# One table of expert slots in DRAM, results scattered by token and choice

## Chip, core, metric

The kernel runs on one core of a Trainium2 chip. The metric is the device time of one execution in microseconds (us). The core has TensorE (PE; matmuls and transposes into PSUM), VectorE (DVE), ScalarE (ACT), GpSimd (POOL) and SyncE (SP). DMAs are issued from SP, ACT and POOL; those whose rows are chosen by an index (gathers and scatters) are issued from POOL.

## What is computed

A decoder layer for 512 tokens of width 1024. After a mixer (recurrent branch and dilated attention) and a layer norm, a mixture of 32 experts is applied, of which each token uses four; then a layer norm, a gated embedding and a last layer norm. The part that matters here:

```python
def _moe(x, w_router, b_router, w_gate, b_gate, w_up, b_up, w_down, b_down):
    logits = (xt @ w_router).astype(jnp.float32) + b_router.astype(jnp.float32)
    top_v, top_e = lax.top_k(logits, TOP_K)
    gates = jax.nn.softmax(top_v, axis=-1)
    ...
        g = xe @ w_gate[e] + b_gate[e]
        up = xe @ w_up[e] + b_up[e]
        g = jnp.minimum(g, SWIGLU_LIMIT)
        up = jnp.clip(up, -SWIGLU_LIMIT, SWIGLU_LIMIT)
        hdn = (up + 1.0) * (g * jax.nn.sigmoid(SWIGLU_ALPHA * g))
        return hdn @ w_down[e] + b_down[e]
    ...
    y = jnp.zeros((T, D), jnp.float32).at[buf_tok].add(yb.astype(jnp.float32) * buf_w[:, None])
```

## The kernel before

Up to about 650 us stand the mixer, the first layer norm and the router. The normed rows are written to a table `tab` in DRAM. `cum` (32 experts x 512 tokens) holds the running count of each expert's tokens, so that the token in slot i of an expert is the number of tokens whose count is at most i.

The experts are taken in pairs, ranked by their number of tokens: an even place holds up to 128 tokens, an odd ("small") place up to 64, packed so that the high and low halves of the operands share one pass. Every expert has three stages, gate, up and down, of four quarters each (`times`, L1035). A quarter needs a megabyte of weights that ACT and DVE have split into a high and a low part (`split_ahead`, L1001, `hi_lo`, L69); up to four split pairs lie ahead of PE, and each split frees a slot for which SP issues the next load (`load_next`, L635). The stages run in the order up e, gate e+1, down e. Small tasks are hung into the quarters by hand: `plan` (L1294) names a quarter and a task, and the lists `pre` and `post` say whether it is traced ahead of the quarter's split or behind its matmuls. From L1282 on, the instructions of DVE, ACT and PE keep the order in which they are traced; those of POOL and SP are ordered by the scheduler.

Which tokens an expert gets is found expert by expert. `index_mm(e)` (L786) broadcasts the expert's row of `cum` to 128 partitions with one matmul into a PSUM bank; `index(e)` (L790) compares it with the partition's number on DVE and sums, which gives the token of each slot, then casts it to an integer. `gather(e)` (L808) fetches those rows of `tab` with an indirect DMA, two experts ahead of their use (`x_turn`, `x_homes`).

`result(e)` (L1135) copies an expert's output from PSUM to `yh` and writes it to a contiguous block of `yall` in DRAM. The last two experts never go there; their outputs are placed by matmuls with a one-hot matrix (`finish`, `place`). `token_rows` (L1192) computes once, for each token and choice, the row of `yall` that holds its result. At the end `bring` (L1180) gathers, by that row, the results of 128 tokens for one choice at a time (16 indirect DMAs, two to a buffer of 1 MB), and `add` (L1186) adds them into `acc` with their weights: four adds in the last gate stage, four in the last up stage, four in each of the two last down stages (`in_down`, L1417, `in_last`, L1439).

Of the kernel before, what the change touches and what calls it, by code (L numbers as in the profile page):

```python
# [19 lines left out]
S = 512  # L20
# [42 lines left out]
def build(tc, a, out):  # L63
# [29 lines left out]
    dram = top.enter_context(tc.tile_pool(name="dram", bufs=1, space=bass.MemoryType.DRAM))  # L93
    tab = dram.tile([S, D], F32, name="tab")
    gtab = dram.tile([S, E], F32, name="gtab")
    yall = dram.tile([(E // 2 - 1) * (128 + SM), D], F32, name="yall")
    pled = dram.tile([S, D], F32, name="pled")

    phase1 = stack()
# [457 lines left out]
    for p in (0, 64):  # L557
# [10 lines left out]
    V.scalar_tensor_tensor(bdn[96:98], lor[96:98].bitcast(F32), ident[96:98, 97:98], bdn[96:98].bitcast(F32),  # L568
                           op0=OP.mult, op1=OP.add)

    def branch(w, u, src, g, after):
        kt = len(src[1])
        for m in range(2):
            c = slice(m * 128, m * 128 + 128)
            ps = ps_p.tile([128, S], F32, name="pp")
            for k in range(kt):
                mm3(ps, (w[0][:, k, c], w[1][:, k, c]), (src[0][:, k], src[1][k]), k == 0, k == kt - 1)
            V.tensor_tensor(g[2 * u + m], g[2 * u + m], ps, op=OP.mult)
            after(2 * u + m)
# [77 lines left out]
    def bcast(ap, shape):  # L657
        return ap.to_broadcast(shape)
# [119 lines left out]
    def small(e):  # L778
        return e % 2 == 1
# [1 line left out]
    def on_chip(e):  # L781
        return e >= E - 2

    sel, cbs = {}, {}

    def index_mm(e):  # L786
        cbs[e] = ps_y.tile([128, S], F32, name="py")
        T.matmul(cbs[e], bcast(pick[:, e:e + 1], [128, 128]), cum, start=True, stop=True)

    def index(e, cb=None, junk=None):  # L790

        if cb is None:
            cb = junk = cbs.pop(e)
        else:
            T.matmul(cb, bcast(pick[:, e:e + 1] if e else first, [128, 128]), cum, start=True, stop=True)
        pos = mp.tile([128, 1], F32, name="pos", bufs=5)
        V.tensor_scalar(junk, cb, ip2 if small(e) else ip, None, op0=OP.is_le, op1=OP.add, accum_out=pos)
        idx = mp.tile([128, 1], I32, name="idx", bufs=3)
        V.tensor_copy(idx, pos)
        sel[e] = [pos, idx]  # L800

    def fetch(into, src, idx, n=128):

        G.indirect_dma_start(out=into[:n], out_offset=None, in_=src,
                             in_offset=bass.IndirectOffsetOnAxis(ap=idx[:n], axis=0),
                             bounds_check=src.shape[0] - 1, oob_is_err=False)

    def gather(e):  # L808
        idx = sel[e][1]
        if small(e):  # L810
            fetch(xgs, tab, idx, SM)
        else:
            fetch(xg, tab, idx)
        if on_chip(e):
            wtg = mp.tile([128, E], F32, name="wtg", bufs=2)
            G.memset(wtg, 0.0)
            fetch(wtg, gtab, idx)
            sel[e].append(wtg)


    wo = []
# [42 lines left out]
    index(0, ps_r.tile([128, S], F32, name="pg"), rt.tile([128, S], F32, name="xt1", bufs=1))  # L864
    gather(0)


# [205 lines left out]
    def x_homes(e, j):  # L1073

        if j == 0 and on_chip(e):
            wt = mw.tile([128, 1], F32, name="wt")
            junk = mw.tile([128, E], F32, name="oh", bufs=1)
            V.scalar_tensor_tensor(junk, rows[:, 0], float(e), sel[e][2], op0=OP.is_equal, op1=OP.mult, accum_out=wt)
            sel[e][1] = wt
# [52 lines left out]
    def h_small(e):  # L1132
        hT[e] = halves("hh", sg.pop(e), mw)

    def result(e):  # L1135

        ps = psd.pop((e, "d"))
        if small(e):
            y, low = [mw.tile([SM, D], F32, name=name, bufs=1) for name in ("yh", "gs")]
            for h in HS:  # L1140
                A.activation(low[:, h], ps[:, h][SM:], AF.Copy)
            for h in HS:
                V.tensor_tensor(y[:, h], ps[:, h][:SM], low[:, h], op=OP.add)
            G.dma_start(yall[e // 2 * (128 + SM) + 128:e // 2 * (128 + SM) + 128 + SM], y)
        else:
            y = mw.tile([128, D], F32, name="yh", bufs=1)
            for h in HS:
                A.activation(y[:, h], ps[:, h], AF.Copy)
            G.dma_start(yall[e // 2 * (128 + SM):e // 2 * (128 + SM) + 128], y)

    def finish(ps, pos, wt, iS, names=("yh", "gs", "xh")):

# [7 lines left out]
    def down_whole(e, between):  # L1160
        if e == E - 1:
            ps = ps_g.tile([128, D], F32, name="pg")
            names = ("yh", "gs", "xh")
        else:
            ps = TwoBanks([ps_y.tile([128, 512], F32, name="py") for _ in range(2)])
            names = ("hh", "hl", "sg")
        times_whole(ps, hT.pop(e), (e, "d"), between)
        ys[e] = finish(ps, *sel.pop(e)[:2], iS, names)

    def place(ps, e, r, h, first, last):  # L1170

# [8 lines left out]
    def bring(r, k):  # L1180
        n = r * TOP + k
        if n % 2 == 0:
            got[n // 2] = slot(("ringb", "ring")[n // 2 % 2], [128, 2, D])
        fetch(got[n // 2][:, n % 2], yall, yidx[:, n:n + 1])

    def add(r, k):  # L1186
        n = r * TOP + k
        V.scalar_tensor_tensor(acc[:, r], got[n // 2][:, n % 2], evs[:, r, k:k + 1], acc[:, r], op0=OP.mult, op1=OP.add)

    yidx = mp.tile([128, R * TOP], I32, name="yidx")  # L1190

    def token_rows():  # L1192

        cT, far, where = [mw.tile([128, R, E], F32, name=name, bufs=1) for name in ("xh", "hl", "hh")]
        yrow = mw.tile([128, R * TOP], F32, name="gpos", bufs=1)
        tq = ps_y.tile([128, R, E], F32, name="py")
        for r in range(R):  # L1200
            T.transpose(tq[:, r], cum.bitcast(F32)[0:E, r * 128:r * 128 + 128], ident[:E, :E])
        sh = [128, R, E]
        V.tensor_tensor(far, tq, bcast(rows[:, 2:3], sh), op=OP.is_gt)
        V.scalar_tensor_tensor(cT, far, 8192.0, tq, op0=OP.mult, op1=OP.add)
        V.tensor_tensor(cT, cT, bcast(rows[:, 1:2], sh), op=OP.add)
# [4 lines left out]
        V.scalar_tensor_tensor(ev, yrow, yall.shape[0] - 0.5, ev, op0=OP.is_lt, op1=OP.mult)  # L1210
        V.tensor_copy(yidx, yrow)

    def turned_gates():

# [71 lines left out]
        x_homes(0, j)  # L1286
    for _ in range(2):
        split_ahead()
    index_mm(1)
    index(1)  # L1290
    gather(1)
    split_ahead()

    def plan(*tasks):  # L1294

# [24 lines left out]

    gate_mm(0, {}, plan((0, index_mm, 2), (1, index, 2), (1, gather, 2), (2, token_rows), (3, turned_gates)))
    gate_out(0)
    for e in range(E - 1):
        f, last = e + 1, e == E - 2
        pre, post = [], [(1, x_turn, f), (2, gather, e + 2), (2, index_mm, e + 3)]
        if e == 0:
            post = post[:1] + post[2:]
        if e:  # L1330
            pre.append((0, result, e - 1))
        pre.append((2, x_homes, f, 0))
        if not small(f):
            pre.append((3, x_homes, f, 1))
        post = [t for t in post if t[2] < E]
        if last:
            post += [(q, bring, n // TOP, n % TOP) for q in range(4) for n in (2 * q, 2 * q + 1)]
            pre.append((0, first_rows))
        up_mm(e, plan(*pre), plan(*post))

        pre, post = [], []
        if e + 3 < E:
            pre.append((1 if small(e) else 2, index, e + 3))
        if small(e):
            pre += [(0, up_in, e), (2, up_small, e), (3, h_small, e)]
            post += [(0, up_fold, e)]
# [2 lines left out]
            post += [(2, h_turn, e)]  # L1349
        if e == 0:  # L1350
            pre += [(q, scale, q) for q in range(4)]
        if last:
            pre += [(q, add, 0, q) for q in range(4)]
            post += [(q, bring, 2, q) for q in range(4)]
        gate_mm(f, plan(*pre), plan(*post))

        pre, post = [], []
# [6 lines left out]
        if not last:  # L1364
            down_mm(e, plan(*pre), plan(*post))
        else:
            pre += [(q, add, 1, q) for q in range(4)]
            post += [(q, bring, 3, q) for q in range(4)]
            up_mm(f, plan(*pre), plan(*post))

    iS = numbers(xgs[:, 0:S])
# [28 lines left out]

    lns = [ln_rows(("ln2_g", "ln2_b"), "ring2")]
    wg_lo = slot("ring2", WG, F32R)
    plev = rows_of(pled, "ring")
    lns.append(ln_rows(("ln3_g", "ln3_b"), "ring"))
    scratch = slot("ring", [128, 2, D])

    def wg_split(u):
        if u < 2:
            pair = [wp.tile(WG, F32R, name=name) for name in ("whi", "wlo")]
# [7 lines left out]
    def in_down(q):  # L1417
        if q == 0:
            wg_split(0)
        if q == 1:  # L1420
            up_in(E - 1)
            up_fold(E - 1)
            up_small(E - 1)
            hT[E - 1] = halves("xh", sg.pop(E - 1), mr)
        if q == 2:
            wg_split(1)
        add(2, q)

    down_whole(E - 2, in_down)

# [8 lines left out]
    def in_last(q):  # L1439
        if q < 2:  # L1440
            for h in HS:
                bias_rows(sums[q][:, h], q, h)
            wg_split(q + 2)
        elif q == 2:

            A.activation(tiny, epst, AF.Sqrt)
        add(3, q)

    down_whole(E - 1, in_last)


    part = mp.tile([128, 2, R, 2], F32, name="part")
# [132 lines left out]
```

## Time and profile before

| | us |
|---|---|
| median of 3 runs (1870.08 to 1872.62) | 1872.47 |
| the profiled execution | 1869.88 |
| its span, first to last instruction | 1867.7 |
| busy: PE, DVE, ACT, POOL | 1771.9, 1407.6, 1163.3, 151.8 |

Times in the rows count from the span's start. A busy PE is not PE at its peak, since matmuls are pipelined. The chain of waits is followed back from the last instruction, at each step to what released it. Idle time stands in brackets behind an instruction, with what ended it. All calls of DVE, ACT and PE go through one helper and so have line 47; tiles tell them apart. Tiles of the pools `ring` and `ring2` are both shown as ring.

### The profile page before, as it was taken

How to read it: one execution, taken by the hardware profiler on the slowest of the kernel's cores; microseconds unless marked ns; L12 is line 12 of the kernel's file. 1: busy time of each engine (PE TensorE's matmuls, PEld its weight loads, DVE VectorE, ACT ScalarE, POOL GpSimd, SP SyncE). 2: the span in 40 equal slices, each digit the busy share in tenths (PEclk: the TensorE clock that was granted, in tenths of full speed). 3: DMA queues.
4: the chain of work that ended last, by engine and by line, in shares of the span. 5: the costliest groups of instructions: out<-in, count | busy, mean ns of one | idle time of the engine just before them, and what ended most of it. 6: DMA issues, size and time to landing. Idle time of an engine off the chain costs nothing.

```text
span 1867.7 us, 23225 instructions
## 1 busy us (share of the span) xinstructions
PE 1771.9 (95%) x8610; PEld 1458.6 (78%) x8610; DVE 1407.6 (75%) x1473; ACT 1163.3 (62%) x1165; POOL 151.8 (8%) x119
## 2 busy tenths in 40 slices
PE   8999999999999789999999999999999999998898
PEld 7989888888879667777778778778778778777567
DVE  4233333466667598999999999999999999998765
ACT  3233345465533377778778778778778778777334
POOL 1010100000000011001010010000100100112400
PEclk9999999999999899999999999999999999999899
DMA  6322221132346479999999999999999999999931
GB/s 180 91 69 68 69 68 57 49 111 80 99 138 237 167 289 360 378 400 386 382 395 385 395 387 385 390 384 390 395 382 390 386 381 395 378 390 362 356 122 46
DMA packets 138352, 503.03 MB, mean 269 GB/s; under 512 B 11347, under 2 KB 77861, under 8 KB 89076
## 3 DMA queue, kind: packets, MB, share of 16 engines
q1 hardware_dynamic: 127076, 470.62, 66.9%
q0 software_dynamic: 9856, 28.39, 4.1%
q10 hardware_dynamic: 1296, 2.43, 0.3%
q8 instruction: 70, 1.15, 0.3%
q14 instruction: 54, 0.44, 0.1%
HBM read 487.73 MB, written 18.22 MB: 271 GB/s over the span
## 4 chain that ended last, share of the span: by engine, by line
PE 52%; DVE 25%; issue 14%; ACT 5%; DMA 3%; another core or an unknown queue 0%; POOL 0%; DVEq 0%; SPq 0%; ACTq 0%; POOLq 0%
PE pp L47 22%; DVE wlo L47 13%; PE py L47 10%; PE pu L47 8%; PE pg L47 5%; DVE ringb L47 4%; PE pt L47 4%; ACT ringb L47 3%; PE s L47 2%; PE o L47 1%; DVE py L47 1%; DVE pu L47 1%; DVE yh L47 1%; DMA wraw<-in_w_ple_gate_dram 1%; DVE xh L47 1%
## 5 line engine op out<-in xcount | busy, mean ns | idle before, releaser
L47 DVE TENSOR_TENSOR wlo<-ring,whi 128x2048 fp32r<-128x2048 f32 x237 | 537.7, 2285 | 29.0 <-ACT whi L47 28.7
L47 ACT ACTIVATE whi<-ring 128x2048 fp32r<-128x2048 f32 x237 | 449.3, 1915 | 79.6 <-PE pg L47 37.7
L47 DVE TENSOR_TENSOR wlo<-wraw,whi 128x1024 fp32r<-128x1024 f32 (+2 forms) x139 | 225.2, 1626 | 164.1 <-ACT whi L47 164.0
L47 ACT ACTIVATE whi<-wraw 128x1024 fp32r<-128x1024 f32 (+2 forms) x139 | 190.2, 1381 | 129.1 <-PE pp L47 104.4
L47 PE MATMUL pp<-xth,whi 128*128 128x512 f32 x448 | 180.8, 404 | 0.0
L47 PE MATMUL pp<-xtl,whi 128*128 128x512 f32 x448 | 175.4, 391 | 0.0
L47 PE MATMUL pp<-xth,wlo 128*128 128x512 f32 x448 | 174.9, 391 | 0.2 <-DVE wlo L47 0.2
L47 PE MATMUL pu<-whi,xh 128*128 128x512 f32 (+1 forms) x440 | 140.3, 391 | 0.4 <-ACT xh L47 0.4
L47 PE MATMUL pg<-whi,xh 128*128 128x512 f32 (+1 forms) x420 | 134.6, 396 | 4.0 <-ACT whi L47 4.0
L47 PE MATMUL pg<-wlo,xh 128*128 128x512 f32 (+1 forms) x412 | 131.0, 395 | 5.0 <-DVE wlo L47 5.0
L47 PE MATMUL pu<-wlo,xh 128*128 128x512 f32 (+1 forms) x424 | 132.6, 388 | 3.0 <-DVE wlo L47 3.0
L47 DVE TENSOR_TENSOR ringb<-ring,ringb 128x2048 fp32r<-128x2048 f32 x45 | 103.1, 2290 | 30.3 <-ACT ringb L47 30.3
L47 PE MATMUL py<-whi,hh 128*128 128x512 f32 x364 | 118.2, 406 | 2.2 <-DVE hh L47 0.3
L47 PE MATMUL py<-wlo,hh 128*128 128x512 f32 x364 | 115.4, 398 | 1.2 <-DVE wlo L47 1.1
L47 DVE TENSOR_TENSOR ringb<-wraw,ringb 128x2048 fp32r<-128x2048 f32 x46 | 105.2, 2286 | 12.7 <-ACT ringb L47 12.7
L47 PEld LDWEIGHTS pp<-xtl,whi 128*128 128x128 f32 x448 | 84.7, 189 | 19.8 <-issue 2.9
L47 PEld LDWEIGHTS pp<-xth,whi 128*128 128x128 f32 x448 | 84.6, 189 | 18.5
L47 PEld LDWEIGHTS pp<-xth,wlo 128*128 128x128 f32 x448 | 84.3, 188 | 18.6 <-DVE wlo L47 0.7
L47 PEld LDWEIGHTS pg<-wlo,xh 128*128 128x128 f32 x412 | 78.6, 191 | 23.8 <-DVE wlo L47 6.2
L47 PEld LDWEIGHTS pu<-wlo,xh 128*128 128x128 f32 x424 | 79.5, 188 | 22.0 <-DVE wlo L47 4.3
L47 PEld LDWEIGHTS pg<-whi,xh 128*128 128x128 f32 x420 | 78.8, 191 | 21.2 <-ACT whi L47 4.6
L47 PEld LDWEIGHTS pu<-whi,xh 128*128 128x128 f32 x440 | 80.3, 188 | 16.2 <-ACT xh L47 0.6
(422 smaller groups left out, 3419.8 us busy)
## 6 DMA issues: line engine op xcount, KB each, us to landing
ring<-in_w_gate_dram SPq DMA_DIRECT2D x98, 1024.0 KB, 7.3
ring<-in_w_down_dram SPq DMA_DIRECT2D x96, 1024.0 KB, 7.5
ring<-in_w_up_dram SPq DMA_DIRECT2D x94, 1024.0 KB, 7.8
wraw<-in_w_up_dram SPq DMA_DIRECT2D x34, 1024.0 KB, 7.1
wraw<-in_w_down_dram SPq DMA_DIRECT2D x32, 1024.0 KB, 8.7
wraw<-in_w_gate_dram SPq DMA_DIRECT2D x30, 1024.0 KB, 7.5
wraw<-in_w_in_dram SPq DMA_DIRECT2D x18, 1024.0 KB, 5.1
wraw<-in_w_in_dram SPq DMA_DIRECT2D x32, 512.0 KB, 4.2
```

What stands on the lines that cost most here:

```text
L47: ins = method(*args, **kw)
```

## The change

A DRAM table `stab` with one entry for each slot of each expert (16 pairs x 192 slots) is filled with the number 2048, which is no row, and 16 indirect DMAs (`fill`, one for each block of 128 tokens and choice) scatter into it, by the slot's number, the row `token * 4 + choice`. `slot_rows` reads the table back into `slotn`, 128 slots x 32 experts, with three DMAs of four-byte pieces, and one DVE shift makes the tokens, `toks`. `gather` takes its indices from `toks` for experts 4 and up; for 0 to 3 the search stays (`direct`). `token_rows` moves from quarter 2 to quarter 0 of the first gate stage, the fills stand behind quarter 1, `slot_rows` behind quarter 2 of the first up stage.

The results go to `ytok`, one row for each token and choice, which is filled with zeros ahead of the mixer's last products. `store` scatters an expert's output to those rows with an indirect DMA. `bring` becomes a plain DMA of two choices of 128 tokens, 1 MB. The adds move: four in the last up stage, four in the down stage of expert 30, eight in that of expert 31; the loads for the end (`plev`, the last norm's rows) and the scratch buffer come behind that.

```diff
-    yall = dram.tile([(E // 2 - 1) * (128 + SM), D], F32, name="yall")
+    ytok = dram.tile([S * TOP, D], F32, name="ytok")
+    stab = dram.tile([E // 2 * (128 + SM), 1], I32, name="stab")
...
+    zero = bt.tile([128, D], F32, name="zero")
+    G.memset(zero, 0.0)
+    for n in range(S * TOP // 128):
+        G.dma_start(ytok[n * 128:n * 128 + 128], zero)
+    none = bt.tile([128, stab.shape[0] // 128], I32, name="none")
+    G.memset(none, S * TOP)
+    G.dma_start(stab.rearrange("(p n) o -> p (n o)", p=128), none)
...
-    def index_mm(e):
-        cbs[e] = ps_y.tile([128, S], F32, name="py")
-        T.matmul(cbs[e], bcast(pick[:, e:e + 1], [128, 128]), cum, start=True, stop=True)
...
     def gather(e):
-        idx = sel[e][1]
+        idx = sel[e] if e in sel else toks[:, e:e + 1]
...
+    def store(e, y, n):
+        G.indirect_dma_start(out=ytok, out_offset=bass.IndirectOffsetOnAxis(ap=slotn[:n, e:e + 1], axis=0),
+                             in_=y, in_offset=None, bounds_check=S * TOP - 1, oob_is_err=False)
...
-            G.dma_start(yall[e // 2 * (128 + SM) + 128:e // 2 * (128 + SM) + 128 + SM], y)
+            store(e, y, SM)
...
-        fetch(got[n // 2][:, n % 2], yall, yidx[:, n:n + 1])
+            G.dma_start(got[n // 2], ytok.rearrange("(r i k) d -> r i k d", r=R, k=TOP)[r][:, k:k + 2])
...
+    def fill(n):
+        G.indirect_dma_start(out=stab, out_offset=bass.IndirectOffsetOnAxis(ap=srow[:, n:n + 1], axis=0),
+                             in_=rown[:, n:n + 1], in_offset=None, bounds_check=stab.shape[0] - 1, oob_is_err=False)
+
+    def slot_rows():
+        v = stab.rearrange("(j c) o -> c (j o)", c=128 + SM)
+        pairs_ = slotn.rearrange("p (j t) -> p j t", t=2)
+        G.dma_start(pairs_[:, :, 0], v[0:128])
+        for rows_ in (slice(0, SM), slice(SM, 128)):
+            G.dma_start(pairs_[rows_, :, 1], v[128:])
+        V.tensor_scalar(toks, slotn, 2, None, op0=OP.logical_shift_right)
+
+    def position(e):
+        poss[e] = mp.tile([128, 1], F32, name="pos", bufs=2)
+        V.tensor_copy(poss[e], toks[:, e:e + 1])
...
-    gate_mm(0, {}, plan((0, index_mm, 2), (1, index, 2), (1, gather, 2), (2, token_rows), (3, turned_gates)))
+    gate_mm(0, {}, plan((0, token_rows), *[(1, fill, n) for n in range(R * TOP)], (1, direct, 2), (1, gather, 2),
+                        (2, direct, 3), (3, turned_gates)))
...
-        pre, post = [], [(1, x_turn, f), (2, gather, e + 2), (2, index_mm, e + 3)]
+        pre, post = [], [(1, x_turn, f), (2, gather, e + 2)]
         if e == 0:
-            post = post[:1] + post[2:]
+            post = post[:1] + [(2, slot_rows)]
...
-        if e + 3 < E:
-            pre.append((1 if small(e) else 2, index, e + 3))
...
-        if last:
-            pre += [(q, add, 0, q) for q in range(4)]
-            post += [(q, bring, 2, q) for q in range(4)]
         gate_mm(f, plan(*pre), plan(*post))
...
-            pre += [(q, add, 1, q) for q in range(4)]
-            post += [(q, bring, 3, q) for q in range(4)]
+            pre += [(q, add, 0, q) for q in range(4)]
+            post += [(q, bring, 2, q) for q in range(4)]
             up_mm(f, plan(*pre), plan(*post))
...
-        add(2, q)
+        add(1, q)
+        bring(3, q)
...
-        add(3, q)
+        for n in (2 * q, 2 * q + 1):
+            add(2 + n // TOP, n % TOP)
 
     down_whole(E - 1, in_last)
+    scratch = slot("ring", [128, 2, D])
+    plev = rows_of(pled, "ring")
+    lns.append(ln_rows(("ln3_g", "ln3_b"), "ring"))
```

## Rows read from the trace of the kernel before

**Rows 1.** Windows: length; busy (count) of PE, PEld, DVE, ACT, POOL; clock, DMA share, GB/s

```profile
855.76:1607.69 751.93, 719.04 (x3367) 583.29 (x3367) 701.81 (x485) 585.41 (x452) 64.65 (x44) 1.00 1.00 388
```

**Rows 2.** The page's part 4, the chain that ended last, whole run

```profile
PE 52%; DVE 25%; issue 14%; ACT 5%; DMA 3%; another core or an unknown queue 0%; POOL 0%; DVEq 0%; SPq 0%; ACTq 0%; POOLq 0%
```

**Rows 3.** Timeline of DVE, one pair: start, duration, engine, line, operation, tiles

```profile
1416.77 0.76 DVE L47 TENSOR_SCALAR_CACHE_REDUCE py<-py,ip 128x512 f32<-128x512 f32 x1
...
1417.70 2.29 DVE L47 TENSOR_TENSOR wlo<-ring,whi 128x2048 fp32r<-128x2048 f32 x1
...
1453.62 0.75 DVE L47 TENSOR_SCALAR_CACHE_REDUCE py<-py,ip 128x512 f32<-128x512 f32 x1
...
1454.57 2.29 DVE L47 TENSOR_TENSOR wlo<-ring,whi 128x2048 fp32r<-128x2048 f32 x1
1456.78 0.68 DVE L47 TENSOR_TENSOR hl<-pt,hh 128x512 fp32r<-128x512 f32 x1
```

**Rows 4.** Timeline of PE, the same pair

```profile
1408.30 0.40 PE L47 MATMUL py<-cum,pick 128*128 128x512 f32 x1
1408.54 2.01 PE L47 MATMUL pu<-ringb,xh 128*128 128x512 f32 x8
...
1424.18 0.73 PE L47 MATMUL py<-whi,hh 128*128 128x512 f32 x2 [0.15 <-DVE hh L47]
...
1457.52 0.73 PE L47 MATMUL py<-whi,hl 128*128 128x512 f32 x2 [1.96 <-DVE hl L47]
```

**Rows 5.** Timeline of DVE, the first expert's gate and up stages

```profile
666.36 2.28 DVE L47 TENSOR_TENSOR ringb<-ring,ringb 128x2048 fp32r<-128x2048 f32 x1
...
673.90 0.28 DVE L47 TENSOR_TENSOR hl<-py,rows 128x128 f32<-128x128 f32 x1
...
677.63 2.28 DVE L47 TENSOR_TENSOR wlo<-wraw,whi 128x2048 fp32r<-128x2048 f32 x1
...
685.67 4.48 DVE L47 TENSOR_TENSOR wlo<-ring,whi 128x2048 fp32r<-128x2048 f32 x2
```

**Rows 6.** Timeline of POOL, DMA issues: attention, first gathers, the end

```profile
132.09 0.96 POOL L309 DMA_DIRECT2D d<-st  x1
...
134.73 0.54 POOL L311 DMA_DIRECT2D other<-d  x1 [0.64 <-DMA d<-st]
...
664.83 2.46 POOL L804 DMA_INDIRECT xgs<-tab,idx  x1 [21.46 <-DVE idx L47]
...
1717.58 1.39 POOL L804 DMA_INDIRECT ringb<-yall,yidx  x1 [3.67 <-DMA yall<-yh]
...
1721.55 0.99 POOL L804 DMA_INDIRECT ringb<-yall,yidx  x1 [0.30 <-issue]
1722.85 0.99 POOL L804 DMA_INDIRECT ringb<-yall,yidx  x1 [0.31 <-issue]
```

**Rows 7.** DMA issues: KB each, median us from issue to landing

```profile
wraw<-in_w_out_dram SPq DMA_DIRECT2D x4, 1024.0 KB, 5.1
...
d<-st POOLq DMA_DIRECT2D x8, 8.0 KB, 2.2
...
wtg<-gtab,idx POOLq DMA_INDIRECT x2, 7.7
```

**Rows 8.** Windows, as rows 1: where the zeros would be written

```profile
500.00:520.00 20.00, 20.00 (x90) 16.57 (x89) 17.90 (x20) 10.89 (x12) 0.00 (x0) 1.00 0.48 152
```

**Rows 9.** The end: timelines of DVE and PE, and one window

```profile
1723.89 1.28 DVE L47 SCALAR_TENSOR_TENSOR acc<-ringb,evs,acc 128x1024 f32<-128x1024 f32 x1 [2.21 <-DMA ringb<-yall,yidx]
...
1787.70 2.61 DVE L47 SCALAR_TENSOR_TENSOR acc<-ring,evs,acc 128x1024 f32<-128x1024 f32 x2
1727.44 1.22 PE L47 MATMUL pg<-wlo,xh 128*128 128x512 f32 x2 [3.89 <-DVE wlo L47]
...
1758.37 3.67 PE L47 MATMUL pt<-two,gs 128*128 128x64 f32 x16 [3.64 <-ACT gs L47]
1725.00:1730.00 5.00, 2.56 (x6) 2.05 (x7) 4.97 (x6) 0.00 (x0) 2.94 (x2) 0.62 1.03 398
```

More of the change, by code (lines that the diff above doesn't have):

```diff
@@ L782, in on_chip, with index @@
         return e >= E - 2
-    sel, cbs = {}, {}
-    def index_mm(e):
-        cbs[e] = ps_y.tile([128, S], F32, name="py")
-        T.matmul(cbs[e], bcast(pick[:, e:e + 1], [128, 128]), cum, start=True, stop=True)
[L790 to L800, printed above, removed]
+    sel, wts, poss = {}, {}, {}
+    def index(e, cb):
+        T.matmul(cb, bcast(pick[:, e:e + 1] if e else first, [128, 128]), cum, start=True, stop=True)
+        pos = mp.tile([128, 1], F32, name="pos", bufs=2)
+        V.tensor_scalar(cb, cb, ip2 if small(e) else ip, None, op0=OP.is_le, op1=OP.add, accum_out=pos)
+        sel[e] = mp.tile([128, 1], I32, name="idx", bufs=4)
+        V.tensor_copy(sel[e], pos)
     def fetch(into, src, idx, n=128):
@@ L817, in gather @@
             fetch(wtg, gtab, idx)
-            sel[e].append(wtg)
+            wts[e] = wtg
     wo = []
@@ L863, in build @@
     V.tensor_tensor_scan(cum[0:E], bcast(one, [E, S]), mT, 0.0, OP.mult, OP.add)
-    index(0, ps_r.tile([128, S], F32, name="pg"), rt.tile([128, S], F32, name="xt1", bufs=1))
+    index(0, ps_r.tile([128, S], F32, name="pg"))
     gather(0)
@@ L1077, in x_homes @@
             junk = mw.tile([128, E], F32, name="oh", bufs=1)
-            V.scalar_tensor_tensor(junk, rows[:, 0], float(e), sel[e][2], op0=OP.is_equal, op1=OP.mult, accum_out=wt)
-            sel[e][1] = wt
+            V.scalar_tensor_tensor(junk, rows[:, 0], float(e), wts[e], op0=OP.is_equal, op1=OP.mult, accum_out=wt)
+            wts[e] = wt
+            position(e)
         if small(e):
@@ L1148, in result @@
                 A.activation(y[:, h], ps[:, h], AF.Copy)
-            G.dma_start(yall[e // 2 * (128 + SM):e // 2 * (128 + SM) + 128], y)
+            store(e, y, 128)
     def finish(ps, pos, wt, iS, names=("yh", "gs", "xh")):
@@ L1167, in down_whole @@
         times_whole(ps, hT.pop(e), (e, "d"), between)
[L1168 removed]
+        ys[e] = finish(ps, poss[e], wts[e], iS, names)
     def place(ps, e, r, h, first, last):
@@ L1188, in add @@
         V.scalar_tensor_tensor(acc[:, r], got[n // 2][:, n % 2], evs[:, r, k:k + 1], acc[:, r], op0=OP.mult, op1=OP.add)
-    yidx = mp.tile([128, R * TOP], I32, name="yidx")
+    srow = mp.tile([128, R * TOP], I32, name="srow")
+    rown = mp.tile([128, R * TOP], I32, name="rown")
+    G.iota(rown.rearrange("p (r k) -> p r k", r=R), pattern=[[128 * TOP, R], [1, TOP]], base=0, channel_multiplier=TOP)
+    slotn = mp.tile([128, E], I32, name="slotn")
+    toks = mp.tile([128, E], I32, name="toks")
     def token_rows():
@@ L1209, in token_rows @@
         ev = evs.rearrange("p r k -> p (r k)")
-        V.scalar_tensor_tensor(ev, yrow, yall.shape[0] - 0.5, ev, op0=OP.is_lt, op1=OP.mult)
-        V.tensor_copy(yidx, yrow)
+        V.scalar_tensor_tensor(ev, yrow, (E // 2 - 1) * (128.0 + SM) - 0.5, ev, op0=OP.is_lt, op1=OP.mult)
+        V.tensor_copy(srow, yrow)
+        G.memset(slotn, S * TOP)
+    def fill(n):
[11 more added lines that the diff above has]
+        V.tensor_copy(poss[e], toks[:, e:e + 1])
     def turned_gates():
@@ L1288, in build, with direct @@
         split_ahead()
-    index_mm(1)
-    index(1)
+    index(1, ps_y.tile([128, S], F32, name="py"))
     gather(1)
     split_ahead()
+    def direct(e):
+        index(e, ps_y.tile([128, S], F32, name="py"))
     def plan(*tasks):
@@ L1334, in build @@
             pre.append((3, x_homes, f, 1))
-        post = [t for t in post if t[2] < E]
+        post = [t for t in post if len(t) < 3 or t[2] < E]
         if last:
@@ L1402, in build @@
     wg_lo = slot("ring2", WG, F32R)
-    plev = rows_of(pled, "ring")
-    lns.append(ln_rows(("ln3_g", "ln3_b"), "ring"))
-    scratch = slot("ring", [128, 2, D])
     def wg_split(u):
```

## The prediction

> **What bounds the kernel now.** I read the busy times by window first, then the chain of waits, then the engines' timelines over one pair of experts. In the eleven pairs from 855.76 to 1607.69 us TensorE is busy 719.04 of 751.93 us and VectorE 701.81 [rows 1]: a pair takes 751.93 / 11 = 68.36 us and TensorE idles (751.93 - 719.04) / 11 = 2.99 of it. The chain over the whole run is 52% TensorE and 25% VectorE [rows 2], so the two bind in turn. The timelines say where. From the wait at 1457.52 on, TensorE runs on into the next pair; in the pair shown, it first stops at 1424.18 (0.15 us, for VectorE's hh). From there VectorE has the longer work, up to hl at 1456.78, for which TensorE stops 1.96 us at 1457.52 [rows 3, 4]. An index search that sits in VectorE's part costs its length; one that sits in TensorE's part costs only its matmul. DMA moves 388 GB/s there [rows 1]; that SyncE's loads could go 2% faster is assumed.
>
> **What goes.** 32 searches become four (experts 0 to 3); 28 go, two in each of 14 pairs. On VectorE one goes from 1416.77 to 1417.70 (0.93 us) and the other from 1453.62 to 1454.57 (0.95) [rows 3]; on TensorE one matmul takes 1408.54 - 1408.30 = 0.24 us [rows 4]. By the reading above, per pair: the matmul in TensorE's part, 0.24; the stop at 1424.18, 0.15, since hh comes 0.93 earlier; and the search ahead of hl (1456.78), 0.95. The other search and the other matmul fall into the other engine's part and buy nothing. Sum 1.34 us, times 14 = **19 us off**. Bounds: only the two matmuls count, 0.48 x 14 = 7; everything counts, (0.48 + 1.88) x 14 = 33.
>
> **What is added where the table is made.** It is made once, right behind the first expert's gate. The token rows move from quarter 2 of that stage to quarter 0: VectorE is free for them when the split that starts at 666.36 ends, at 668.6, and they take 677.63 - 673.90 = 3.7 us [rows 5], so the 16 scatters may begin at 672.3. Each is an indirect DMA of 128 four-byte entries on GpSimd, and all write the same DRAM tile through an index. Then three small DMAs bring the table back into slotn, and VectorE's shift makes toks from it. VectorE's instructions keep the order of the program, and the shift stands behind quarter 2 of the first up stage: in the old timeline after the first of the two splits that start at 685.67, at 687.9 [rows 5], plus 0.9 for the search of expert 3 that moves ahead of it, 688.8. So the table has 16.5 us until VectorE stands still, and behind the shift every split of weights is queued: TensorE runs out of split pairs a few microseconds later, SyncE gets no free slot to load into, and nothing else hides the wait. On GpSimd the gather of expert 2 is queued behind the scatters; its rows are needed in the second up stage, which stands behind the shift too.
>
> How long do 16 scatters take? No row shows one write through an index behind another write to the same table. The nearest is a read: the first gather from yall, 1717.58, waited 3.67 us for the last store to land, though its rows could be elsewhere [rows 6]; an access through an index is taken to touch the whole table. I take the same for a write behind a write: each scatter waits for the one before to land. With the weight stream running, a small indirect DMA lands 7.7 us after its start [rows 7]; with little traffic a small write to DRAM and the issue that waits for it lie 134.73 - 132.09 = 2.6 us apart, 0.96 of it GpSimd's [rows 6]. An indirect issue took 2.46 us beside a busy VectorE (664.83) and 0.99 beside an idle one (1721.55) [rows 6]. So: three scatters at 7.7 us, from 672.3 to 695.4; by then VectorE stands, the loads are drained, and 13 scatters go at 3.0 each (2.6, and some of the longer issue), to 734.4. The three reads cost some 0.8 us of issue each and 2.2 to land [rows 7], 4.6 in all: toks can run at 739. VectorE waits 739 - 688.8 = **50 us on**. VectorE is the engine that is late there, so all of it reaches the end. Bounds: 13 x 2.6 in place of 3.0 gives 45; all 16 at the loaded 7.7 gives 16 x 7.7 + 7.7 - 16.5 = 114, which would need the loads to go on while VectorE stands, so I stay near the light rows.
>
> The table is read back in four-byte pieces, 2048 to a DMA. The rows bear on small pieces only so far: d<-st moves 8 KB in pieces of 16 bytes and lands in 2.2 us [rows 7], so I charge nothing for them. The Trainium skill ("DMA: Bandwidth & Descriptors", Rules for kernel authors) speaks against this part: a strided last dimension lowers to one descriptor per element. The trace has nothing as fine to hold against it. The same page (Two DMAs through the same engine are not ordered) wants the issuing engine to wait on the first DMA's semaphore before a dependent one, which is the wait I assume; the trace agrees for reads, with the 3.67 us above. Its fixed cost of about 2.0 us a DMA (Anatomy of one DMA) would by estimate make the 13 scatters 26 us in place of 39, and the time 1887; the trace's 2.2 and 2.6 lie above it.
>
> **What is added elsewhere.** Zeros: 16 writes of 512 KB early on, near 510 us. The stretch from 500 to 520 moves 152 GB/s [rows 8]; with some 240 to spare the 8.4 MB take about 35 us. What hides them is that weights are loaded a unit ahead. I take 1 us; if the cover fails, two loads of w_out, of 5.1 us each [rows 7], are late by their own length: 10.
>
> Stores: an indirect issue (2.46 us) in place of a plain one (up to 0.96) [rows 6], 30 times, on an engine that is busy 64.65 of 751.93 us [rows 1]; the buffer that a store reads is next written one expert, 34 us, later. Nothing; without that cover, 1.5 us an expert. The fills of constants on GpSimd and two small casts on VectorE are nothing either.
>
> The end: the first four adds leave the last gate stage. There VectorE waited 2.21 us for the gathered rows and TensorE 3.89 for VectorE, then ran some 5 us with a mean granted clock of 0.62, so mostly at 1.2 GHz (another 2.5 lost) [rows 9]. Six come back, and perhaps 2 of the 3.64 at 1758.37, since the gathers that slowed that load are spread. But the last down stage holds eight adds in place of four, 1.3 us each (two take 2.61 at 1787.70 [rows 9]), ahead of the matrix that places the last expert: 5 on. Together **3 off**, bounds 10 off (the adds hide in VectorE's waits) and 5 on (nothing comes back). The plain reads in place of 16 indirect ones free GpSimd, which nobody waits for then.
>
> **The sum.** 1869.9 (profiled execution; its span is 1867.7, the rest is launch) - 19 + 50 + 1 - 3 = 1899. The median of the runs shown is 2.6 above the profiled execution, which lies at their lower edge; I say **1900**.
>
> **The rivals.** (a) The scatters do not wait for one another, as the gathers at the end don't: those go out 0.30 us apart (1721.55 + 0.99, then 1722.85 [rows 6]). Then 6 go in the 16.5 us at 2.46 + 0.3, ten more at 1.3, to 702; they land by 706 (4, between 2.2 and 7.7), with the reads 711: VectorE waits 22 us, and 1869.9 - 19 + 22 + 1 - 3 = 1871: no change, 1858 to 1885 by the other terms. This ends on the other side, not slower; it decides at the second scatter, which leaves 0.3 us behind the first's issue or not before that one has landed. For it speaks that the gathers do so, against it that they only read. (b) As (a), with every issue at 0.99 and both searches on the path: 16 x 1.3 to issue, 6.5 for the last landing and the reads, less the 16.5, are 11 on, and 2 x 0.94 + 0.24 = 2.1 a pair, 30 off: 1869.9 + 11 - 30 - 3 = 1848. (c) In line, and the landing stays at its loaded 7.7: 114 on, 1869.9 - 19 + 114 + 1 - 3 = 1963. Against it: SyncE's loads start when VectorE frees a slot. (d) The searches were covered anyway and only the matmuls count: 12 more than the forecast, 1912; part of its range.
>
> **Chances.** Forecast with (d) 0.61, on its own 1880 to 1925; (a) 0.20; (b) 0.12; (c) 0.07. Leaving out (c), most of (b) and a little at both ends of the others, 1857 to 1928 should hold eight times in ten. A measurement of this kernel can tell 0.2%, 3.7 us, from no change. Faster by more: (b) and less than half of (a), 0.20. Within it: 0.07. Slower: the rest of (a), the forecast, (c): 0.73.
>
> **What the profile after would show.** Sixteen indirect issues on GpSimd from about 672 us, each idle until the one before has landed, 7 to 8 us apart at first and then about 3; a VectorE hole of some 50 us ahead of one small shift, with TensorE idle and the DMA rate near zero in it; pairs of 67.0 us in place of 68.4; the wait for hl near 1 us in place of 1.96; no stop of TensorE in the last gate stage and VectorE's adds ending some 5 us later against the last matmul of the down stage. If the scatters stand 0.3 us apart, step two falls and (a) or (b) holds; if the pairs stay at 68 us, step one falls; if the hole is over 60 us, the loads did not drain.

## The result, and the profile after

The changed kernel took 1893.43 us (median of 4 runs, 1891.99 to 1895.45); the kernel before, measured beside it, 1871.28 (4 runs). The ratio is 1.0121, with a 95% interval of 1.0109 to 1.0134: 22 us slower, where the prediction said 1900 (1857 to 1928) and slower. Every run of the changed kernel lies above every run of the kernel before. The profiled execution took 1891.99, its span is 1890.3.

Where the 22.6 us between the two spans (1867.7 and 1890.3) came from is read from the result stores of even experts. First the store of expert 0 and that of expert 28, kernel before, then after (GpSimd's timeline):

```profile
719.10 0.59 POOL L1149 DMA_DIRECT2D yall<-yh  x1 [16.15 <-ACT yh L47]
...
1676.02 0.59 POOL L1149 DMA_DIRECT2D yall<-yh  x1 [10.45 <-ACT yh L47]
```

```profile
757.31 1.21 POOL L1139 DMA_INDIRECT ytok<-yh,slotn  x1 [22.96 <-ACT yh L47]
...
958.29 1.20 POOL L1139 DMA_INDIRECT ytok<-yh,slotn  x1 [21.31 <-ACT yh L47]
...
1695.25 1.20 POOL L1139 DMA_INDIRECT ytok<-yh,slotn  x1 [21.32 <-ACT yh L47]
```

| stretch | before | after | difference |
|---|---|---|---|
| start to store of expert 0 | 719.1 | 757.3 | +38.2 |
| 14 pairs, to store of expert 28 | 956.9 | 937.9 | -19.0 |
| from there to the end | 191.7 | 195.1 | +3.4 |

A pair takes 937.94 / 14 = 67.00 us. Eleven of them, from 958.29 on (windows, as [rows 1]), and TensorE's waits in them (what was waited for, us in total, times, longest):

```profile
958.29:1695.25 736.96, 711.41 (x3345) 580.08 (x3345) 681.58 (x419) 586.64 (x452) 147.83 (x44) 1.00 1.00 391
```

```profile
PE pt L47 <- DVE sg L47: 14.7, 11, 1.3
PE py L47 <- DVE hl L47: 10.8, 11, 1.0
```

The same view of the kernel before, over the eleven pairs of [rows 1]:

```profile
PE py L47 <- DVE hl L47: 21.5, 11, 2.0
PE pt L47 <- DVE sg L47: 9.8, 11, 1.1
```

The stop for hl, 1.96 us in [rows 4], is 1.0, and VectorE is busy 20 us less than in [rows 1] for as many pairs. The stop for sg has grown, from 9.8 to 14.7 us: it lies in VectorE's part, and time that TensorE saves there, as with the second matmul of a pair, turns into waiting. That fits the sum, which put nothing on it.

The 38 us at the start come from one hole. GpSimd's timeline shows the 16 scatters into `stab`; in brackets stands what each waited for:

```profile
670.06 2.82 POOL L1226 DMA_INDIRECT stab<-rown,srow  x1 [5.34 <-DVE srow L47]
678.24 1.01 POOL L1226 DMA_INDIRECT stab<-rown,srow  x1 [5.35 <-DVE wlo L47]
...
684.70 2.44 POOL L1226 DMA_INDIRECT stab<-rown,srow  x1 [2.53 <-DMA stab<-rown,srow]
692.10 0.99 POOL L1226 DMA_INDIRECT stab<-rown,srow  x1 [4.96 <-DMA stab<-rown,srow]
694.56 0.98 POOL L1226 DMA_INDIRECT stab<-rown,srow  x1 [1.47 <-DMA stab<-rown,srow]
...
721.93 0.98 POOL L1226 DMA_INDIRECT stab<-rown,srow  x1 [1.43 <-DMA stab<-rown,srow]
724.37 1.24 POOL L1233 DMA_DIRECT2D slotn<-stab  x1 [1.46 <-DMA stab<-rown,srow]
725.60 1.71 POOL L1235 DMA_DIRECT2D slotn<-stab  x2
```

In the second row the view names VectorE's wlo, but that scatter too waits for the one before: by the trace the first has landed at 677.97, and the second leaves at 678.24; in the run one_late (below) the view names the landing for the same link.

VectorE's shift and TensorE's next matmul (timelines), and 30 us in the hole (windows):

```profile
729.66 0.18 DVE L47 TENSOR_SCALAR toks<-slotn 128x32 int32<-128x32 int32 x1 [43.40 <-DMA slotn<-stab]
```

```profile
732.11 1.22 PE L47 MATMUL pg<-wlo,xh 128*128 128x512 f32 x2 [41.49 <-DVE wlo L47]
```

```profile
695.00:725.00 30.00, 0.00 (x0) 0.00 (x0) 0.00 (x0) 0.00 (x0) 12.95 (x14) 0.50 0.04 8
```

Three links of 6.5 to 8.2 us while loads run, then 2.4 us a link (3.1 once, behind the gather of expert 3); meanwhile TensorE, VectorE and ScalarE do nothing and the DMAs move 8 GB/s.

### The profile page after: what moved, and what is told of

The parts are those of the page before. It is cut to its first block, busy times and chain, and to the rows that moved or that the text cites. A ratio compares the mean times of both kernels' runs of the same rounds, so it can differ in the third digit from the quotient of the medians.

```text
span 1890.3 us, 23173 instructions
## 1 busy us (share of the span) xinstructions
PE 1760.5 (93%) x8582; PEld 1452.0 (77%) x8582; DVE 1381.7 (73%) x1392; ACT 1164.6 (62%) x1165; POOL 269.9 (14%) x151
## 4 chain that ended last, share of the span: by engine, by line
PE 37%; DVE 20%; issue 5%; DMA 2%; POOL 1%; ACT 1%; DVEq 0%; POOLq 0%; SPq 0%; ACTq 0%
PE py L47 13%; DVE wlo L47 13%; PE pg L47 11%; PE pu L47 8%; PE pt L47 4%; DVE ringb L47 3%; DVE pu L47 1%; DVE yh L47 1%; DMA wraw<-in_w_ple_gate_dram 1%; DVE acc L47 1%; POOL stab L1226 1%; DVE xh L47 1%; DMA stab<-rown,srow 1%; DMA wraw<-in_w_down_dram 1%; DVE hl L47 1%
## 5 line engine op out<-in xcount | busy, mean ns | idle before, releaser
L806 POOL DMA_INDIRECT xgs<-tab,toks x14 | 112.3, 8024 | 376.3 <-PE pt L47 376.0
L1139 POOL DMA_INDIRECT ytok<-yh,slotn x30 | 44.9, 1496 | 386.3 <-ACT yh L47 321.5
```

The source lines that it names most:

```text
L1139: G.indirect_dma_start(out=ytok, out_offset=bass.IndirectOffsetOnAxis(ap=slotn[:n, e:e + 1], axis=0), in_=y, in_offset=None, bounds_check= ...
```

## The experiments

Ratios are to the kernel before, measured beside each batch (its medians: 1870.3 us beside the first four runs of the table, 1868.5 beside one_late, flat4 and flat4_end, 1869.2 beside the others); the changed kernel itself stands at 1.0121.

| run | median, us | ratio, 95% interval |
|---|---|---|
| s_odd: 14 searches of odd experts back | 1912.4 | 1.0222 [1.0205, 1.0239] |
| s_even: 14 searches of even experts back | 1897.3 | 1.0141 [1.0124, 1.0158] |
| d_same: 8 more scatters, same table | 1915.0 | 1.0239 [1.0219, 1.0260] |
| d_own: 8 more scatters, own tables | 1897.3 | 1.0145 [1.0125, 1.0165] |
| one_late: one table, shift later | 1877.0 | 1.0045 [1.0029, 1.0061] |
| four: four tables, merged later | 1859.4 | 0.9945 [0.9928, 0.9961] |
| flat4: as four, read in 128-byte rows | 1852.3 | 0.9919 [0.9902, 0.9936] |
| flat4_end: as flat4, two adds later | 1848.9 | 0.9893 [0.9877, 0.9910] |
| z_twice: zeros written twice | 1906.2 | 1.0191 [1.0172, 1.0210] |
| end_back: adds, reads and last loads at their old stages | 1894.7 | 1.0123 [1.0103, 1.0144] |
| bring_late: reads one stage later | 1898.2 | 1.0152 [1.0135, 1.0169] |

**Which search paid.** The prediction gave the two searches of a pair different prices, by whose part of the pair they sit in. Each half was put back by itself:

```diff
+        back = 0 < e < E - 3 and (e + 3) % 2 == 1      # s_odd; == 0 in s_even
+        if back:
+            post.append((2, search_mm, e + 3))
...
+        if back:
+            pre.append((1 if small(e) else 2, search, e + 3))
```

> The changed kernel with the index searches of the 14 odd experts from 5 to 31 put back where the kernel before had them (matmul in quarter 2 of the up stage, compare and cast in quarter 2 of the next gate stage), and their gathers taking them. By the prediction's reading these sit in VectorE's part of a pair, ahead of hl: 0.95 each, 13.3 in all, pair 67.95 us, time 1893.4 + 13.3 = 1906.7, wait for hl near 1.95 us a pair. Rival 1 (both searches of a pair count alike): 19 / 2 = 9.5, time 1902.9. Rival 2 (only the matmuls count): 0.24 x 14 = 3.4, time 1896.8.

> The changed kernel with the index searches of the 14 even experts from 4 to 30 put back (matmul in quarter 2 of the up stage, compare and cast in quarter 1 of the next gate stage). By the prediction's reading these sit in TensorE's part of a pair: the matmul 0.24 and the stop for hh 0.15 each, 5.5 in all, pair 67.39 us, time 1893.4 + 5.5 = 1898.9. Rival 1 (both searches of a pair count alike): 9.5, time 1902.9. Rival 2 (this one costs its full 0.93 + 0.24): 16.4, time 1909.8.

The even ones: 3.9 us more by the medians, 4.9 when each is taken against the kernel before beside it (5.5 expected), and the trace gives (1705.83 - 762.49) / 14 = 67.38 us a pair, 67.39 expected. That trace is of the slowest of the four runs (1903.2 us); what it has beyond the pairs lies mostly ahead of the first store, 5.2 us. The odd ones: ten of the 14 pairs take 67.97 us (the stores of experts 7, 9 and 11 stand at 997.60, 1065.57 and 1133.54), 67.95 expected, with the hl stop at 1.96 again. Both fit the reading: 0.38 and 0.97 us a pair, 1.35 together, as much as left with both (68.35 to 67.00); the rivals fall. But the time with the odd ones was 5.7 us over the expectation. The trace has 17.0 us in the pairs, 3.4 more than 14 x 0.97, most of it in two pairs of 69.49 us. Windows and TensorE in one of these:

```profile
1210.00:1220.00 10.00, 8.44 (x40) 6.38 (x38) 9.90 (x11) 6.18 (x4) 2.06 (x2) 1.00 1.00 412
1220.00:1230.00 10.00, 8.49 (x38) 7.14 (x39) 8.84 (x6) 7.23 (x7) 1.70 (x1) 0.83 0.99 337
```

```profile
1221.51 1.09 PE L47 MATMUL py<-whi,hl 128*128 128x512 f32 x2 [1.96 <-DVE hl L47]
```

Behind that stop the same two matmuls take 1.09 us, in [rows 4] 0.73: the granted clock is 0.83 for ten microseconds, so part of them at 1.2 GHz in place of 2.4. Why two pairs and not the others, with the same stop, stays open. The other microseconds lie ahead of the first store (1.6) and behind expert 28 (2.9).

**What the line is.** Is it the write behind a write to one table, or the scatters as such?

```diff
-    *[(1, fill, n) for n in range(R * TOP)]
+    *[(1, fill, n) for n in [*range(R * TOP), *range(8)]]                                  # d_same
+    *[(1, fill, n) for n in range(R * TOP)], *[(1, spare, n) for n in range(8)]            # d_own
```

> The changed kernel with eight more scatters behind the sixteen: blocks 0 to 7 again, the same values into the same table. Theory (each scatter through an index waits for the one before on its table to land): eight more links of 2.42 us in the light part of the line, VectorE's hole 43.4 + 19.4 = 62.8 us, time 1893.4 + 19.4 = 1912.8. Rival 1 (the line is set by something that ends at a fixed time, the draining loads or the first gathers): hole 43 to 46, time 1893 to 1896. Rival 2 (GpSimd's issue alone counts, 0.98 + 0.3 us): +10, time 1904.

> The changed kernel with eight more scatters of the same blocks, each into a spare table of its own that nobody reads. Theory: they wait for no scatter before them, slip into the waits of the line, and leave 0.3 to 3 us apart; the line of the sixteen is not longer. Hole 43 to 50 us, time 1893 to 1900. Rival (a scatter of 128 entries keeps the DMA queue or GpSimd busy for 2.42 us wherever it writes): hole 62.8, time 1912.8, the same as with eight more into the one table.

Into the same table: hole 63.2 us, against 43.4, so (63.2 - 43.4) / 8 = 2.5 us for each more (2.42 expected; the time, 1915.0, is 2.2 over the theory); both rivals fall. Into tables of their own: hole 48.0. GpSimd there:

```profile
670.76 2.82 POOL L1227 DMA_INDIRECT stab<-rown,srow  x1 [5.34 <-DVE srow L47]
673.89 2.78 POOL L1231 DMA_INDIRECT spare<-rown,srow  x1 [0.30 <-issue]
676.97 2.80 POOL L1231 DMA_INDIRECT spare<-rown,srow  x1 [0.30 <-issue]
...
685.32 2.49 POOL L1227 DMA_INDIRECT stab<-rown,srow  x1 [0.30 <-issue]
```

The spare ones leave 0.3 us after one another. They add 4.6 us, since they hold GpSimd when the second link of the line could have left (685.32 here, 678.24 above). It is the shared table that makes the line. The wait is one that the program has GpSimd take ahead of each issue; no run drops it and keeps the one table.

**Moving the wait, and breaking the line.** In one_late the shift is moved, some 45 us on, and the first result store behind it, and the table comes back in two reads in place of three; in four there are also four tables, scatter n going to table n mod 4, with two reads each, and VectorE merges them. In flat4 an entry's row is slot x 32 + expert, so that a table is read as 128 rows of 128 bytes.

```diff
+        if f == 2:
+            post.append((1, merge_slots))            # one_late, four, flat4: gate stage of expert 2
...
-        G.indirect_dma_start(out=stab, ...
+        G.indirect_dma_start(out=stabs[n % NT], ...  # four, flat4: NT = 4
...
+        for t in range(1, NT):
+            V.tensor_tensor(slotn, part_n[0] if t == 1 else slotn, part_n[t], op=OP.min)
...
-        V.tensor_tensor(cT, cT, bcast(rows[:, 1:2], sh), op=OP.add)
+        V.scalar_tensor_tensor(cT, cT, float(E), bcast(rows[:, 1:2], sh), op0=OP.mult, op1=OP.add)  # flat4
...
+            G.dma_start(part_n[t], stabs[t].rearrange("(c e) o -> c (e o)", e=E))                   # flat4
```

> The changed kernel with its one table, but the shift that makes the tokens, and the first result store behind it, in quarter 1 of the gate stage of expert 2, where the kernel with four tables has its merge (the small reads are two DMAs in place of three). Theory (the line of 16 goes at its loaded pace, 6.5 to 8.2 us a link, as long as VectorE is not waiting): at about 733, when VectorE comes to the shift, some eight or nine links are done; two more at the loaded pace, five at 2.42, the reads 5: VectorE waits to about 765, a hole of some 32 us, time 1893.4 - 43.4 + 32 + 2 = 1884. Rival (moving the wait back by 45 us is enough, four tables were not needed): no hole, 1852 to 1859.

> The changed kernel with four slot tables in place of one: scatter n goes into table n mod 4, each table is read back with two DMAs, VectorE takes the minimum of the four (three small instructions) and the shift, and this stands in quarter 1 of the gate stage of expert 2, some 50 us after the first up stage; the first result store stands behind it. Theory: four scatters are under way at a time, the 16 take some 40 us under load, to about 712, the reads to about 725, before VectorE comes to the merge at about 735. So no hole: the stretch from the first gate stage to the first result store is back near its length before the change, 719, and the time is 1893.4 - 43.4 + 2 = 1852, 1 per cent under the kernel before. Rival 1 (the small pieces, 16384 of 4 bytes, take their time from the loads or land late): a hole of 10 to 20 us at the merge, 1862 to 1872. Rival 2 (the time is bound by the bytes that the DMAs move, and the hole only moved slack): 1885 to 1893.

> The kernel with four slot tables, with another order of the entries: row = slot x 32 + expert, so that each table is read back with one DMA of 128 bytes to a partition in place of two of 4-byte pieces (512 pieces in place of some 16000); the row numbers come from the same three instructions with other constants. With the 4-byte pieces VectorE waited 2.8 and 4.0 us at the merge, and the DMAs moved only 207 GB/s from 720 to 740 us. Theory (the pieces fill the DMA queues): both waits go, the rate stays near 400, time 1859.4 - 6.8 = 1852 to 1853, or a few less. Rival (the reads land late because they stand behind weight loads, whatever their pieces): 1858 to 1860.

With one table the wait is only shorter, 28.19 us (32 expected; the time is 7 us under the theory). As long as VectorE does not stand still, the line goes at its loaded pace, nine links of 6.3 to 8.0 us. The ninth and tenth scatter, the next one, and VectorE's shift (two timelines):

```profile
728.65 2.47 POOL L1233 DMA_INDIRECT stab<-rown,srow  x1 [5.07 <-DMA stab<-rown,srow]
736.37 0.98 POOL L1233 DMA_INDIRECT stab<-rown,srow  x1 [5.25 <-DMA stab<-rown,srow]
738.78 0.98 POOL L1233 DMA_INDIRECT stab<-rown,srow  x1 [1.43 <-DMA stab<-rown,srow]
```

```profile
758.45 0.18 DVE L47 TENSOR_SCALAR toks<-slotn 128x32 int32<-128x32 int32 x1 [28.19 <-DMA slotn<-stab]
```

With four tables the scatters leave 0.30 us apart, the line is gone, and what is left are the reads: the merge waits 6.8 us for them, and the time is 7.4 us over the theory's 1852, 2.6 under rival 1's range. The second scatter of four, and VectorE's merge:

```profile
675.80 2.78 POOL L1233 DMA_INDIRECT stab<-rown,srow  x1 [0.30 <-issue]
...
732.58 0.18 DVE L47 TENSOR_TENSOR slotn<-part,part 128x32 int32<-128x32 int32 x1
735.58 0.19 DVE L47 TENSOR_TENSOR slotn<-slotn,part 128x32 int32<-128x32 int32 x1 [2.82 <-DMA part<-stab]
739.80 0.19 DVE L47 TENSOR_TENSOR slotn<-slotn,part 128x32 int32<-128x32 int32 x1 [4.02 <-DMA part<-stab]
```

The DMA issues (KB each, median us to landing) of four, and its window over the reads; then that window in flat4:

```profile
stab<-rown,srow POOLq DMA_INDIRECT x16, 7.6
part<-stab POOLq DMA_DIRECT2D x8, 8.0 KB, 13.4
```

```profile
720.00:740.00 20.00, 17.43 (x84) 14.06 (x83) 12.90 (x11) 11.30 (x9) 4.35 (x4) 1.00 1.02 207
```

```profile
720.00:740.00 20.00, 19.82 (x93) 16.01 (x92) 18.80 (x17) 16.32 (x14) 6.13 (x5) 1.00 1.01 414
```

The DMA engines are as busy in both (1.02 and 1.01), but beside the 4-byte pieces they move half the bytes. It is not the reads' own packets that fill the time: in the trace of four these are 256 of 256 bytes, 21 of the engines' 328 us in this window, while a packet of 8192 bytes, of which the weight loads consist, takes 610 ns on the mean, in flat4 317. How the pieces slow the others the trace doesn't show. In 128-byte rows the merge waits for nothing, and the median is 7.1 us lower, as expected, though the two intervals overlap a little (and the reads are four in place of eight). This is the rule that the prediction took from the Trainium skill ("DMA: Bandwidth & Descriptors", Rules for kernel authors) and priced at nothing for want of a row: a strided last dimension, one descriptor per element. The runs agree that such reads are dear beside a weight stream, with 207 against 414 GB/s; descriptors they don't show. In the changed kernel itself, where the loads had drained, pricing them at nothing was nearly right: the three reads took 5.3 us, 4.6 in the sum.

**The zeros.**

```diff
-    for n in range(S * TOP // 128):
+    for n in 2 * list(range(S * TOP // 128)):
```

> The changed kernel with the 16 writes of zeros done twice, 16.8 MB in place of 8.4. Theory (the zeros cost nothing, weights are loaded a unit ahead, and a write of zeros waits for an earlier one on its own): within 1 us of 1893.4, the matmuls behind it start where they did. Rival (the zeros take the time of loads that somebody waits for): up to 10 us, 1903.

The rival held, with some 13 us in place of its 10. TensorE's longest waits between 520 and 600 us in z_twice, then in the changed kernel:

```profile
PE pp L47 <- ACT whi L47: 5.3, 1, 5.3
PE pp L47 <- DVE wlo L47: 2.4, 4, 1.0
```

```profile
PE pp L47 <- DVE wlo L47: 1.0, 1, 1.0
PE pp L47 <- DVE ring L47: 0.9, 1, 0.9
```

All waits of that view come to 9.7 and 1.9 us. The granted clock, full there in the changed kernel, is 0.77 from 570 to 580 us in z_twice and 0.89 up to 590. The running count `cum` starts at 647.1 us in z_twice, at 636.5 before, and between 635.5 (the changed kernel) and 640.4 in all the others, 637.4 on the mean of the eleven with one lot of zeros. So the first 8.4 MB cost about 1 us, within the scatter, but they use the cover up: ScalarE waited 17.1 us for w_rnn_out there, in the kernel before not once between 490 and 600 us, and TensorE felt none of it until the second lot.

**The end.**

```diff
# end_back: the adds and reads in the stages of the kernel before
+            pre += [(q, add, 0, q) for q in range(4)]
+            post += [(q, bring, 2, q) for q in range(4)]
         gate_mm(f, plan(*pre), plan(*post))
# bring_late: two of the first four reads one stage later, and so on
-            post += [(q, bring, n // TOP, n % TOP) for q in range(4) for n in (2 * q, 2 * q + 1)]
+            post += [(q, bring, 0, q) for q in range(4)]
# flat4_end: of the last block, choices 0 and 1 behind add_sums(2)
-        for n in (2 * q, 2 * q + 1):
-            add(2 + n // TOP, n % TOP)
+        add(2, q)
+        if q > 1:
+            add(3, q)
```

> The changed kernel with the adds, the reads of results and the loads for the end put back into the stages where the kernel before had them (four adds in the last gate stage, four in the last up stage, four in each of the last two down stages); the reads stay plain. Theory: the last down stage gets back the 4.3 us of its eight adds, but the last gate stage waits again for the first read, which now leaves only at 1741 us: 3.9 and 2.5 us as before the change, and some 4 more since the scatter of expert 29 lands later than the plain store did. Together +6, time 1899. Rival 1 (the move of the adds is what cost the end its 3.4 us): 1890. Rival 2 (the two cancel): 1893.

> The changed kernel with the reads of results one stage later: two MB in the up stage of expert 30, two in that of expert 31, two in the down stage of expert 30, two in that of expert 31 (where the changed kernel has four, two and two); the adds stay. Theory (the load of w_ple_gate landed 16.9 us after its issue, 4.4 more than before, because four MB of results are read beside it): it lands in about 12, TensorE waits 3.6 in place of 8.0 behind it, time 1889 to 1890. Rival 1 (the load is slowed by SyncE's own weight loads): no change there, 1893.4. Rival 2 (the last reads come too late for the last adds): slower, 1895 to 1900.

> The kernel with four tables read in 128-byte rows, and two of the eight adds of the last down stage (the last block's first two choices) moved behind the sums of the third block, where VectorE waits 4.62 us for the turned columns. Theory: the matrix that places the last expert comes 2.6 us sooner, TensorE waits for it 4.4 us in place of 7.0, and the two adds hide: 2.6 off the kernel without this edit, 1849 to 1850. Rival (the adds are then late for something else behind them, the loads for the last norm among it): no gain, 1852.

TensorE's four stops in the end of the changed kernel, and the last of them before the change:

```profile
1743.20 0.73 PE L47 MATMUL pg<-wlo,xh 128*128 128x512 f32 x2 [0.40 <-DVE wlo L47]
...
1774.46 3.68 PE L47 MATMUL pt<-two,gs 128*128 128x64 f32 x16 [8.00 <-ACT gs L47]
...
1794.74 3.70 PE L47 MATMUL pg<-wraw,xh 128*128 128x512 f32 x8 [2.25 <-DMA wraw<-in_w_down_dram]
...
1813.77 0.77 PE L47 MATMUL pu<-yh,xh 128*128 128x512 f32 x1 [7.06 <-DVE xh L47]
```

```profile
1790.85 0.61 PE L47 MATMUL pu<-yh,xh 128*128 128x512 f32 x1 [2.78 <-DVE xh L47]
```

The four in end_back, then in bring_late:

```profile
1754.08 1.22 PE L47 MATMUL pg<-wlo,xh 128*128 128x512 f32 x2 [8.48 <-DVE wlo L47]
...
1786.35 3.68 PE L47 MATMUL pt<-two,gs 128*128 128x64 f32 x16 [5.41 <-ACT gs L47]
...
1803.26 3.70 PE L47 MATMUL pg<-wraw,xh 128*128 128x512 f32 x8 [0.55 <-DMA wraw<-in_w_down_dram]
...
1817.99 0.47 PE L47 MATMUL pu<-yh,xh 128*128 128x512 f32 x1 [2.76 <-DVE xh L47]
```

```profile
1745.66 0.73 PE L47 MATMUL pg<-wlo,xh 128*128 128x512 f32 x2 [0.40 <-DVE wlo L47]
...
1773.77 3.68 PE L47 MATMUL pt<-two,gs 128*128 128x64 f32 x16 [4.84 <-ACT gs L47]
...
1796.17 6.45 PE L47 MATMUL pg<-wraw,xh 128*128 128x512 f32 x8 [5.04 <-DMA wraw<-in_w_down_dram]
...
1817.94 0.76 PE L47 MATMUL pu<-yh,xh 128*128 128x512 f32 x1 [7.07 <-DVE xh L47]
```

With the old stages the first stop is back at 8.48 (3.9 and some 4 more, as expected), the last falls by 4.3, and the two stops in between are shorter, 4.3 together, which was not expected: the ratio is that of the changed kernel, rival 2. With later reads the wait behind w_ple_gate falls from 8.00 to 4.84, so the reads do slow that load; but the load of w_down, which they now run beside, costs 5.04 in place of 2.25. The time was no better, rather some 5 us worse, of which the trace shows 2 behind expert 28. That is the time of rival 2 but not its mechanism, since the last stop is 7.07 as it was.

These stretches scatter. Nine traces with the same instructions from expert 28 on (the changed kernel and the eight runs that leave the end alone) take 192.8 to 198.0 us from that store to the end, 194.9 on the mean, where the one trace of the kernel before has 191.7. In these nine the stop behind w_ple_gate is 7.3 to 8.7 us (3.64 before), the one for w_down 0.9 to 4.3 (none before), the last 7.0 to 7.1; the 4.84 of bring_late and the 2.76 of end_back lie well outside. So the change makes the end longer by 1 to 6 us, and the experiments moved single stops, but the whole stretch hardly beyond its scatter (end_back 196.6, bring_late 196.8). flat4_end comes nearest, with 192.4: its last stop is 5.0 in place of 7.0 (2.6 less expected), and the median is 3.4 below flat4. The ratios' intervals of the two overlap a little, their runs don't. It is the fastest of all: 1.07% under the kernel before.

## Why the prediction was right

The two large terms were right in mechanism, and the trace shows them one by one. That the sum came so near is luck in part: it had 29 us on, the spans have 22.6, because the head came out 12.8 us below its two terms (38.2 against 50 + 1) and the end 6.4 above its own (3.4 on against 3 off).

- **What goes, 19 off:** 18.98 measured, a pair 67.00. s_even and s_odd confirm the two prices, 0.38 and 0.97 us a pair (0.39 and 0.95 in the sum). The price came from TensorE's stops and from which engine has the longer work between them, not from busy shares.
- **The table, 50 on:** hole 43.4. The step that decided the sign, a scatter through an index waits for the one before on the same table, was an analogy with one read in [rows 6], and no row of before could show it for writes; d_same, d_own and four do. Three links at the loaded pace and 13 light ones is what the trace has. The three took 22.0 us (670.06 to 692.10), 23.1 in the sum; the 13 light ones 32.3 (to 724.37), not 39: this is the term that was mis-sized. A link is 2.4 us there, issue included, so nothing had to be put on the 2.6 of [rows 6]. The reads took 5.3 (to 729.66), not 4.6, and the time until VectorE stands was 16.2, not 16.5. Fills and hole both began some 2 us sooner than assumed, since in this trace the first turn of expert 0 did; in that of d_same they began at 672.65 and 688.8, where the sum has 672.3 and 688.8. The gather of expert 2 did not queue behind the scatters, as the prediction had it, but went out between them (679.55), and that of expert 3 too (695.84).
- **The head is 38.2 longer, 5.2 less than the hole.** That all of the hole reaches the end was too much. 2.6 of the difference is the earlier start. The rest lies between the hole and the store: there VectorE waited 1.66 and 2.25 us for ScalarE in the kernel before, and 1.41 in the changed one, 2.5 less.
- **The zeros, 1 on:** nothing in this trace, 0.9 on the mean of eleven against the one before. The reason was right, its margin was not known: 10 us was put on the failure of the cover, and with twice the bytes it was 13.
- **The end, 3 off:** 3.4 on. The stop in the last gate stage did go, 3.89 to 0.40, and the eight adds cost 7.06 - 2.78 = 4.3, near the 5 of the sum. Wrong was the step that gave back 2 of the 3.64 at w_ple_gate because "the gathers that slowed that load are spread": four plain reads of 1 MB are under way beside it, about as many bytes as the gathers before, the load takes 16.9 us (issued 1754.51, ScalarE begins on it at 1771.53), and the stop is 8.00. bring_late shows that these reads are part of it; what the rest is stays open. And the sum had no term for w_down, for which TensorE now stops 2.25 us.
- **Rivals.** (a) and (b) needed scatters 0.3 us apart. That is what four has, with the wait moved as well, and there the change is faster than the kernel before; with one table no link is under 2.4 us. (c) needed the landing to stay loaded while VectorE stands. The links fell to 2.4 within one link of the stop; one_late shows the loaded pace going on for nine links while VectorE works. (d) falls with s_odd.

## What to carry to other kernels

Before a set of small indirect writes goes to one table, ask what orders them: here each waited for the one before, and 16 with their reads made a hole of 43 us in which TensorE, VectorE and ScalarE stood. Moving the wait by 45 us hid only 15 of them, since under load a link takes three times as long; separate tables and a small merge, with the wait moved, hid all but 6.8. Lay a table out so that it is read back in rows, not in 4-byte pieces: beside a weight stream such pieces cost far more than their bytes.

## What was not expected of the hardware

- Reads in 4-byte pieces slow the DMAs beside them: 2048 pieces to a DMA, landing after 13.4 us (median of 8), while all DMAs together moved 207 GB/s, in flat4 414 over the same window at the same busy share.
- An indirect issue on GpSimd took from 0.92 to 9.94 us in the changed kernel, 0.98 while VectorE stood still; what makes the long ones was not tested. GpSimd is busy 269.9 us, before 151.8, with single gathers such as the first of these rows in every pair; TensorE never waits for them.

```profile
860.16 8.57 POOL L806 DMA_INDIRECT xgs<-tab,toks  x1 [28.90 <-PE pt L47]
869.03 0.93 POOL L1139 DMA_INDIRECT ytok<-yh,slotn  x1 [0.30 <-issue]
```

- After the hole the granted clock is 0.50 from 730 to 735 us and 0.78 to 0.84 up to 745, so TensorE, which had stopped for 41.49 us, starts again at 1.2 GHz; and in two pairs of s_odd it was 0.83 behind a stop of 2 us that elsewhere left it at full.
